# A decoder layer on one core: three sets of transposes moved from TensorE to VectorE's 32x32 turns and the stores behind them

## The chip, the core and the metric

The kernel runs on one core of a Trainium2 chip. The metric is the device time of one execution in microseconds, median of several runs. A core has TensorE (PE; its weight loads are listed as PEld), VectorE (DVE), ScalarE (ACT), GpSimd (POOL), and SyncE (SP), which here only issues DMAs. All data lie in SBUF, in PSUM (where TensorE writes) or in the chip's HBM. All arithmetic is float32; a product of float32 operands is made of three products of rounded parts (high times high, high times low, low times high).

## The reference, cut to what matters

One decoder layer, sequence 1024, width 1024. One projection feeds two groups of heads; their outputs are joined, projected, added to the input, and followed by a squared-ReLU MLP.

```python
h = rms_norm(x, norm1_w); proj = h @ w_in
# group A: 4 heads of differential attention, values of 128
da_o = (softmax(q1 k1^T) - lam * softmax(q2 k2^T)) v
da_o = rms_norm(da_o, da_out_norm_w) * (1.0 - lam_init)
# group B: 4 heads of the gated delta rule on convolved q, k, v (128 each)
dn_o = gated_delta_rule(dn_q, dn_k, dn_v, g, beta)
dn_o = rms_norm(dn_o, dn_out_norm_w) * silu(dn_z)
mix = concatenate([da_o, dn_o])            # (1024 tokens, 512 + 512)
x = x + mix @ w_out
x = x + square(relu(rms_norm(x, norm2_w) @ w_up)) @ w_down
```

## The kernel before

Tokens are cut into 8 tiles (or chunks) of 128. A matrix that is the operand of a projection is kept with features on partitions and tokens along them, as a rounded high part `hH` and a remainder `hL`, both [128, 8, 1024]. So whatever is computed with tokens on partitions has to be turned before a projection, and the other way round.

**Delta rule, projections** (50 to 250 us). `dn_proj(kind)` makes keys, queries and values, in this order, with features on partitions and 512 tokens at a time, convolves them on VectorE (L682) and yields 8 groups (4 heads, 2 halves). For the values (L851 to L857), `transposed` turns a group by four TensorE transposes into a bank of PSUM (L716); VectorE multiplies it by a factor of each token, `vsc`, on the way out (L854), and `park` stores it into slot 2 of the HBM tensor `park_d` with one DMA on SP. Between these groups, `horner` inverts the triangular matrices; its `V.transpose` (L806) turns 32x32 blocks.

**Delta rule, scan** (250 to 350 us). `scan` runs over the 8 chunks. `load` brings slots 0 to 2 of `park_d` for four heads into the tile `pka`, of which there are two, so the loads run about a chunk ahead. Each chunk is a chain: product with the state (L918), VectorE's combination with the values in slot 2 (L922), product with the inverse (L930), ScalarE's copy (L932), product for the new state (L941), VectorE's update (L947). In chunk 0 the values go into L930 directly. `scan_out` makes the chunk's output: two products (L970, L977), then mean square, power (L291 on GpSimd), gate and norm (L989), and a store to `mixn_d` from GpSimd's queue (L991). The gate comes in the tile `zgt`, of which there is one.

**Order of work.** In the scan, the attention and the output projection, TensorE's instructions keep the order in which the program issues them. That order is made by a planner, `Interleave`: generators (`scan`, `values`, `scores`, `da_turns`, `da_units`, `mixed`, `outproj` and others) each yield the time at which their next step should be ready and the bank of PSUM that they need, and the planner runs, of those that are ready, the one of highest priority. Its clock advances by given costs of TensorE (`flow.pe`), and `flow.chain` reckons when a row of instructions on the other engines will be done; `flow.hold` marks a bank as taken until then. The orders of the other engines and of the DMA queues are chosen by the compiler's scheduler. The scan starts at 18 us of the planner's clock; the projections of the attention (`da_units`) fill TensorE around it, and `da_turns` turns their rows.

**Attention** (350 to 580 us). For head and token tile, `scores` makes the exponentials, and `values` turns them (L1238), multiplies them with the values (L1250) into a bank of the pair `px`, copies the result (L1259), squares it into the same bank (L1260), and scales it (L1264) by mean square and weight. Heads 0 and 1 run over all tiles first and store each [128, 128] block to `mixa_d` from GpSimd's queue (L1266). Heads 2 and 3 follow tile by tile, and write into a row tile `mx` whose first half is loaded from `mixa_d` (L1231).

**Towards the output projection.** `mix_loads` loads the delta rule's rows into the tile `mt` (L1295), and `mixed` takes each row tile, of either group, through `turn` and `to_hT`: four TensorE transposes into a bank of `px` (L298), ScalarE's rounding into `hH` (L303), VectorE's remainder into `hL` (L304). `outproj` multiplies the delta rule's half and then the attention's (L1340 to L1342). The MLP follows and isn't touched.

Of the kernel before, what the change touches and what calls it, by code (L numbers as in the profile page):

```python
# [18 lines left out]
P = 128  # L19
# [96 lines left out]
def powr(n):  # L116
    return "G", 180.0 + 285.0 * n
# [3 lines left out]
def tile_hymba_layer(  # L121
# [46 lines left out]

    zg_d = dram.tile([NT, P, 512], F32, name="zg_d")
    park_d = dram.tile([HEADS, NT, P, 5, P], F32, name="park_d")  # L170
    mixn_d = dram.tile([NT, P, 512], F32, name="mixn_d")
    mixa_d = dram.tile([NT, P, 256], F32, name="mixa_d")
    fsx_d = dram.tile([P, 1024], F32, name="fsx_d")
    fsg_d = dram.tile([P, 1024], F32, name="fsg_d")
    qk_d = dram.tile([2, 2, NT, P, 2, 2 * P], F32, name="qk_d")
# [525 lines left out]
    def park(h, hf, slot, src):  # L701
        nc.sync.dma_start(park_d[h, 4 * hf:4 * hf + 4, :, slot, :].rearrange("c p d -> p c d"), v4(src))

    def cols4(t, h, hf):
        return t[:, 8 * h + 4 * hf:8 * h + 4 * hf + 4]

    def bc_col(t):
        return t.unsqueeze(2).broadcast_to([P, 4, P])
# [4 lines left out]
    def transposed(src):  # L713
        ps = pt_.tile([P, 512], F32, tag="pt", name="ps_t")
        for c in range(4):
            T.transpose(ps[:, c * P:(c + 1) * P], src[:, c * P:(c + 1) * P], ident)  # L716
        return ps
# [131 lines left out]

    heads = [((h, h + 1), hf) for hf in range(2) for h in (0, 2)]  # L850
    for h, hf, v2 in skew(dn_proj(2)):  # L851
        ps = transposed(v2)
        vs = ta("kn", 2)
        V.tensor_tensor(v4(vs), v4(ps), bc_col(cols4(vsc, h, hf)), ALU.mult)  # L854
        park(h, hf, 2, vs)
        if hf == 0:
            horner(*heads.pop(0))  # L857

# [43 lines left out]
    def scan():  # L902
        St = {}
        psA = pA.tile([P, 512], F32, name="ps_A")
        PA = {h: psA[:, h * P:(h + 1) * P] for h in range(HEADS)}

        def load(c):
            pka = sb.tile([P, HEADS, 3, P], F32, tag="pka", name="pka", bufs=2)
            for h in range(HEADS):
                nc.sync.dma_start(pka[:, h], park_d[h, c, :, 0:3, :])  # L910
            return pka

        nxt = load(0)
        for c in range(NT):
            pk, rr_, yy = nxt, {}, {}
            if c > 0:
                for h in range(HEADS):
                    T.matmul(PA[h], pk[:, h, 0, :], St[h], start=True, stop=True)  # L918
                for h in range(HEADS):
                    i = cidx(h, c)  # L920
                    rr_[h] = sb.tile([P, P], F32, tag="sr", name="sr", bufs=4)
                    V.scalar_tensor_tensor(rr_[h], PA[h], neg_eg[:, i:i + 1], pk[:, h, 2, :], ALU.mult, ALU.add)  # L922
                flow.pe(4 * MM)
                yield flow.chain(*[vec(P, 60)] * 4), None
            else:
                for h in range(HEADS):
                    rr_[h] = pk[:, h, 2, :]
            for h in range(HEADS):
                Wc = W[h, c // 4][:, (c % 4) * P:(c % 4 + 1) * P]
                T.matmul(PA[h], Wc, rr_[h], start=True, stop=True)  # L930
            y4 = sb.tile([P, 512], F32, tag="sy", name="sy", bufs=2)
            S.copy(y4, psA)  # L932
            if c + 1 < NT:
                nxt = load(c + 1)
            flow.pe(4 * MM)
            yield flow.chain(act(512)), None
            Sold = dict(St)
            for h in range(HEADS):
                yy[h] = y4[:, h * P:(h + 1) * P]
                if c < NT - 1:  # L940
                    T.matmul(PA[h], pk[:, h, 1, :], yy[h], start=True, stop=True)  # L941
            if c < NT - 1:
                for h in range(HEADS):
                    i = cidx(h, c)
                    Sn = sb.tile([P, P], F32, tag=f"S{h}", name=f"S{h}", bufs=2)
                    if c > 0:
                        V.scalar_tensor_tensor(Sn, St[h], elast[:, i:i + 1], PA[h], ALU.mult, ALU.add)  # L947
                    else:
                        V.tensor_copy(Sn, PA[h])
                    St[h] = Sn  # L950
                flow.pe(4 * MM)
            flow.add(1, scan_out(c, Sold, yy), 0, "pB")
            if c < NT - 1:
                yield flow.chain(*[vec(P, 60)] * 4), None

    def scan_out(c, Sold, yy):
# [29 lines left out]
        rstd(f, so, 1.0 / P, EPS, sb, "oft", 4)  # L986
        V.tensor_tensor(f, f, rq[:, c::8], ALU.mult)
        for h in range(HEADS):
            V.scalar_tensor_tensor(oc[:, h * P:(h + 1) * P], oc[:, h * P:(h + 1) * P], f[:, h:h + 1],  # L989
                                   zgt[:, h * P:(h + 1) * P], ALU.mult, ALU.mult)  # L990
        nc.gpsimd.dma_start(mixn_d[c], oc)  # L991
        flow.pe(4 * MM)
        t = flow.chain(vec(512))
        flow.hold("pB", t)
        flow.chain(*[act(P, True)] * 4, vec(4), powr(4), vec(4), *[vec(P, 60)] * 4, start=t)
        if c == NT - 1:
            s2ctx.close()
            spctx.close()
# [223 lines left out]
    def values():  # L1222
        for _ in order:
# [40 lines left out]
            V.scalar_tensor_tensor(om, om, f, dawb, ALU.mult, ALU.mult)  # L1264
# [5 lines left out]
            t = flow.chain(act(P, True), vec(1), powr(1), vec(1), vec(P, 60), start=t)  # L1270
# [5 lines left out]
    landed, hns = {}, {}  # L1276

    def turn(r, src, t, tb, k0, keep=None):
        to_hT(src, tb, lambda: bank_tile(px, r, "ps_tr"), k0, 4, keep)
# [638 lines left out]
```

## Time and profile before

| | |
|---|---|
| median of 3 runs | 1234.14 us (1233.48 to 1234.69) |
| the profiled execution | 1234.74 us, span 1233.0 us |
| granted clock of TensorE | 1.000 |
| DMA packets, bytes | 143301, 202.12 MB |
| HBM read, written | 135.86 MB, 65.01 MB |

The profile is of one execution. Its span runs from the first to the last instruction; the execution's own time has 1.7 us around it. The page gives the busy time of each engine, the chain of work that ended last (followed back from the last instruction, at each step to what released it), and groups of instructions by line. In the answers of the trace, a row such as "DVE STREAM_TRANSPOSE W<-gb x8: 690/702/712" gives the engine, the operation, the tile written and the one read, the count, and the least, median and greatest duration in ns. Rows of the chain and of the timeline begin with the start and the duration in us.

### The profile page before, as it was taken

To read this page: it belongs to the slowest core of one execution; us is meant where nothing else is said; L and a number is where in the kernel's file an instruction comes from. 1 tells how busy PE (TensorE), PEld (TensorE's weight loads), DVE (VectorE), ACT (ScalarE), POOL (GpSimd) and SP (SyncE) were. 2 spreads that over 40 slices of the span, in tenths; PEclk is the share of its full clock that TensorE was granted. 3 is DMA by queue.
4 is the path that set the end of the run, shared out by engine and by line. 5 is a ranking of instruction groups with operands and counts; after the bars stand their busy time and mean duration, and the time that the engine had idled before them with its cause. 6 is when DMAs were issued, how large, how long until landed. Compare 5 with 4: busy or idle time off the path is not lost.

```text
span 1233.0 us, 18819 instructions
## 1 busy us (share of the span) xinstructions
PE 1217.3 (99%) x6823; PEld 1054.3 (86%) x6823; DVE 824.7 (67%) x1524; ACT 624.2 (51%) x1249; POOL 151.3 (12%) x215
## 2 busy tenths in 40 slices
PE   9999999999999999999999999999999999999998
PEld 8978888898999998888888888888888888888886
DVE  6868796556647657777799544565569755777543
ACT  6588553344346555566666544444564333333330
POOL 2411110043434421001200000000000000000000
PEclk9999999999999999999999999999999999999999
DMA  9344653278748756323437434444479645423301
GB/s 350 98 115 122 163 162 104 63 234 240 231 148 252 232 162 159 85 77 108 157 117 255 172 122 151 171 170 153 155 241 382 234 179 184 163 103 103 137 35 69
DMA packets 143301, 202.12 MB, mean 164 GB/s; under 512 B 20920, under 2 KB 98280, under 8 KB 143208
## 3 DMA queue, kind: packets, MB, share of 16 engines
q1 hardware_dynamic: 138584, 187.28, 46.9%
q0 software_dynamic: 4480, 13.64, 2.9%
q8 instruction: 54, 0.88, 0.3%
q14 instruction: 39, 0.32, 0.1%
q10 hardware_dynamic: 144, 0.00, 0.0%
HBM read 135.86 MB, written 65.01 MB: 163 GB/s over the span
## 4 chain that ended last, share of the span: by engine, by line
PE 88%; DVE 4%; DMA 3%; ACT 2%; issue 2%; POOL 1%; SPq 1%; POOLq 0%; DVEq 0%; ACTq 0%
PE X L1517 4%; PE X L1515 4%; PE X L1516 4%; PE X L1814 4%; PE X L1815 4%; PE X L1813 4%; PE ps_dn L265 3%; PE ps_dn L267 3%; PE ps_dn L266 3%; PE ps_qk L1067 3%; PE ps_qk L1068 3%; PE ps_qk L1069 3%; PE ps_o L1250 2%; PE Y L1515 2%; PE Y L1517 2%; PE Y L1516 2%
## 5 line engine op out<-in xcount | busy, mean ns | idle before, releaser
L1433 ACT CAST hH<-ur 128x1024 fp32r<-128x1024 f32 x56 | 58.9, 1051 | 173.4 <-PE Y L1814 89.8
L1434 DVE TENSOR_TENSOR hL<-ur,hH 128x1024 fp32r<-128x1024 f32 x56 | 68.3, 1223 | 79.4 <-ACT hH L1433 79.4
L1067 PE MATMUL ps_qk<-wH,hH 128*128 128x256 f32 x384 | 114.3, 298 | 0.0
L1069 PE MATMUL ps_qk<-wH,hL 128*128 128x256 f32 x384 | 108.7, 283 | 0.0
L1068 PE MATMUL ps_qk<-wL,hH 128*128 128x256 f32 x384 | 108.4, 282 | 0.0
L1434 DVE TENSOR_TENSOR op<-raw,op 128x1024 fp32r<-128x1024 f32 x48 | 58.7, 1223 | 74.2 <-PE X L1516 41.1
L1813 PE MATMUL X<-hH 128*128 128x512 f32 x224 | 87.1, 389 | 0.0
L1814 PE MATMUL X<-hL,hH 128*128 128x512 f32 x224 | 87.1, 389 | 0.0
L1815 PE MATMUL X<-hH,hL 128*128 128x512 f32 x224 | 87.1, 389 | 0.0
L265 PE MATMUL ps_dn<-hH,wH 128*128 128x512 f32 x192 | 76.3, 397 | 0.2 <-ACT cp L678 0.2
L267 PE MATMUL ps_dn<-hH,wL 128*128 128x512 f32 x192 | 75.8, 396 | 0.0
L266 PE MATMUL ps_dn<-hL,wH 128*128 128x512 f32 x192 | 75.8, 395 | 0.0
L1068 PEld LDWEIGHTS ps_qk<-wL,hH 128*128 128x128 f32 x384 | 73.4, 191 | 0.2
L1067 PEld LDWEIGHTS ps_qk<-wH,hH 128*128 128x128 f32 x384 | 73.3, 191 | 0.2
L1069 PEld LDWEIGHTS ps_qk<-wH,hL 128*128 128x128 f32 x384 | 73.1, 190 | 0.0
L1434 DVE TENSOR_TENSOR hL<-dw,hH 128x1024 fp32r<-128x1024 f32 x56 | 68.2, 1218 | 0.9 <-ACT hH L1433 0.9
L1433 ACT CAST op<-raw 128x1024 fp32r<-128x1024 f32 x48 | 50.4, 1052 | 35.7 <-PE Y L1517 19.9
L1433 ACT CAST hH<-dw 128x1024 fp32r<-128x1024 f32 x56 | 58.7, 1048 | 10.7 <-DMA dw<-in_w_down_dram 5.0
L1205 ACT ACTIVATE pexp<-pexp,mx 128x128 f32<-128x128 f32 (+7 forms) x64 | 49.7, 777 | 25.1 <-DVE mx L1204 24.5
L682 DVE SCALAR_TENSOR_TENSOR cy<-cp,pv,cy 128x512 f32<-128x512 f32 x72 | 53.7, 747 | 8.1 <-ACT cy L680 7.3
L1340 PE MATMUL ps_op<-wH,hH 128*128 128x512 f32 x128 | 53.0, 414 | 0.0
L1515 PE MATMUL Y<-hH,op 128*128 128x512 f32 x128 | 49.9, 390 | 0.4 <-DVE ua L1555 0.4
(370 smaller groups left out, 3429.1 us busy)
## 6 DMA issues: line engine op xcount, KB each, us to landing
ur<-ud SPq DMA_DIRECT2D x28, 1024.0 KB, 5.0
raw<-in_w_up_dram SPq DMA_DIRECT2D x32, 512.0 KB, 3.9
dw<-in_w_down_dram SPq DMA_DIRECT2D x32, 512.0 KB, 6.8
wraw<-in_w_units_dram SPq DMA_DIRECT2D x48, 256.0 KB, 3.7
qk_d<-qa POOLq DMA_DIRECT2D x32, 256.0 KB, 4.3
ud<-ua SPq DMA_DIRECT2D x16, 512.0 KB, 4.2
ud<-s SPq DMA_DIRECT2D x16, 512.0 KB, 2.7
pka<-park_d SPq DMA_DIRECT2D x32, 192.0 KB, 4.8
```

What stands on the lines that cost most here:

```text
L265: T.matmul(ps, lh(k), rh(k), start=(k == 0), stop=False)
L266: T.matmul(ps, lh(k), rl(k), start=False, stop=False)
L267: T.matmul(ps, ll(k), rh(k), start=False, stop=(k == n - 1))
L1067: T.matmul(ps[:, :256], hH[:, k, sl], wh[:, k, :], start=(k == 0), stop=False)
L1068: T.matmul(ps[:, :256], hH[:, k, sl], wl[:, k, :], start=False, stop=False)
L1069: T.matmul(ps[:, :256], hL[:, k, sl], wh[:, k, :], start=False, stop=(k == KB - 1))
L1433: S.copy(dst[0], src)
L1434: V.tensor_tensor(dst[1], src, dst[0].bitcast(F32), ALU.subtract)
L1515: T.matmul(ps, op[0][:, k, cs], h[0][:, k, :], start=start and k == 0, stop=False, skip_group_check=True)
L1813: T.matmul(bank[t], v[0][:, j, sl], v[2][:, j], start=s0, stop=False, skip_group_check=True)
L1814: T.matmul(bank[t], v[0][:, j, sl], v[3][:, j], start=False, stop=False, skip_group_check=True)
L1815: T.matmul(bank[t], v[1][:, j, sl], v[2][:, j], start=False, stop=s1, skip_group_check=True)
```

## The change

Three sets of results are turned on VectorE in blocks of 32x32, and a store of four DMAs places the blocks, so that HBM holds the turned matrix.

- Values of the delta rule: `V.transpose` on the group, then `put_blocks` into slot 2 of `park_d`. The factor `vsc` is no longer applied here; GpSimd applies it in the scan, to the loaded tile (`scale`).
- Outputs of the delta rule: L989's result goes into `zgt`, is turned back into `oc`, and stored by `put_blocks` in `mixn_d`, which now has features by tokens. The load brings it with features on partitions, and `settle` rounds it straight into `hH` and `hL`, without a bank or TensorE.
- Attention heads 0 and 1: the scaled block is written into the product's bank, turned from there into `om`, and stored by `put_blocks` in `mixa_d` (features by tokens). When a row tile is complete, `turn_last` rounds its first half directly and turns only the second (heads 2 and 3) on TensorE.
- `put_blocks` issues four DMAs on SP, one for each 32 partitions, in pieces of 32 floats. The stores of `oc` and `om` were on GpSimd's queue before.
- The planner's chains are lengthened by the new VectorE steps; for heads 2 and 3 the bank is now also held through the square.

```diff
-    mixn_d = dram.tile([NT, P, 512], F32, name="mixn_d")
-    mixa_d = dram.tile([NT, P, 256], F32, name="mixa_d")
+    mixn_d = dram.tile([NT, 512, P], F32, name="mixn_d")
+    mixa_d = dram.tile([NT, 256, P], F32, name="mixa_d")
...
+    def put_blocks(dst, src, eng=None):
+        for a in range(4):
+            s = slice(32 * a, 32 * a + 32)
+            (eng or nc.sync).dma_start(dst[:, s].rearrange("(b s) r -> s b r", s=32),
+                                       src[s].rearrange("s (b r) -> s b r", r=32))
...
     for h, hf, v2 in skew(dn_proj(2)):
-        ps = transposed(v2)
         vs = ta("kn", 2)
-        V.tensor_tensor(v4(vs), v4(ps), bc_col(cols4(vsc, h, hf)), ALU.mult)
-        park(h, hf, 2, vs)
+        V.transpose(vs, v2)
+        put_blocks(park_d[h, 4 * hf:4 * hf + 4, :, 2, :].rearrange("c p d -> (c p) d"), vs)
...
+        def scale(c, pk):
+            G.tensor_tensor(pk[:, :, 2, :], pk[:, :, 2, :], bc_col(vsc[:, c::8]), ALU.mult)
+
         nxt = load(0)
+        scale(0, nxt)
...
             flow.add(1, scan_out(c, Sold, yy), 0, "pB")
+            if c + 1 < NT:
+                scale(c + 1, nxt)
...
         for h in range(HEADS):
-            V.scalar_tensor_tensor(oc[:, h * P:(h + 1) * P], oc[:, h * P:(h + 1) * P], f[:, h:h + 1],
-                                   zgt[:, h * P:(h + 1) * P], ALU.mult, ALU.mult)
-        nc.gpsimd.dma_start(mixn_d[c], oc)
+            hs = slice(h * P, (h + 1) * P)
+            V.scalar_tensor_tensor(zgt[:, hs], oc[:, hs], f[:, h:h + 1], zgt[:, hs], ALU.mult, ALU.mult)
+        V.transpose(oc, zgt)
+        put_blocks(mixn_d[c], oc)
...
-                nc.sync.dma_start(rows_of[tb][:, 0:256], mixa_d[tb])
+                nc.sync.dma_start(rows_of[tb][:, 0:256].rearrange("p (k t) -> p k t", k=2),
+                                  mixa_d[tb].rearrange("(k p) t -> p k t", p=P))
...
-            V.scalar_tensor_tensor(om, om, f, dawb, ALU.mult, ALU.mult)
-            if h < 2:
-                nc.gpsimd.dma_start(mixa_d[tb, :, h * P:(h + 1) * P], om)
             flow.pe((tb + 1) * MM)
             t = flow.chain(act(P))
+            if h < 2:
+                V.scalar_tensor_tensor(po[:, 2 * P:3 * P], om, f, dawb, ALU.mult, ALU.mult)
+                V.transpose(om, po[:, 2 * P:3 * P])
+                put_blocks(mixa_d[tb, h * P:(h + 1) * P], om)
+                flow.hold(r, flow.chain(act(P, True), vec(1), powr(1), vec(1), vec(P, 60), vec(P, 60), start=t))
+                continue
+            V.scalar_tensor_tensor(om, om, f, dawb, ALU.mult, ALU.mult)
+            t = flow.chain(act(P, True), start=t)
             flow.hold(r, t)
...
+    def settle(src, tb, ks, t=None):
+        sl = slice(tb * P, (tb + 1) * P)
+        sv = src.rearrange("p (k t) -> p k t", t=P)
+        S.copy(hH[:, ks, sl], sv)
+        V.tensor_tensor(hL[:, ks, sl], sv, hH[:, ks, sl].bitcast(F32), ALU.subtract)
...
+    def turn_last(r, src, t, tb):
+        settle(src[:, 0:256], tb, slice(0, 2))
+        ps = bank_tile(px, r, "ps_tr")
+        for j in (2, 3):
+            T.transpose(ps[:, j * P:(j + 1) * P], src[:, j * P:(j + 1) * P], ident)
+        flow.pe(2 * TR)
+        t = settle(ps[:, 256:512], tb, slice(2, 4))
...
-                nc.sync.dma_start(mt, mixn_d[t])
+                nc.sync.dma_start(mt.rearrange("p (k t) -> p k t", t=P), mixn_d[t].rearrange("(k p) t -> p k t", p=P))
...
+            if x[3] == 4:
+                loads.remove(x)
+                landed[x[2], 4] = settle(x[0], x[2], slice(4, 8))
+                state["mixed"] += 1
+                continue
             r = yield from flow.bank("px")
             loads.remove(x)
-            turn(r, *x)
-            state["mixed"] += x[3] == 4
+            turn_last(r, *x[:3])
```

More of the change, by code (lines that the diff above doesn't have):

```diff
@@ L994, in scan_out @@
         flow.hold("pB", t)
-        flow.chain(*[act(P, True)] * 4, vec(4), powr(4), vec(4), *[vec(P, 60)] * 4, start=t)
+        flow.chain(*[act(P, True)] * 4, vec(4), powr(4), vec(4), *[vec(P, 60)] * 4, vec(512, 100), start=t)
         if c == NT - 1:
@@ L1263, in values @@
             V.tensor_tensor(f, f, ri[:, 0:1], ALU.mult)
-            V.scalar_tensor_tensor(om, om, f, dawb, ALU.mult, ALU.mult)
-            if h < 2:
-                nc.gpsimd.dma_start(mixa_d[tb, :, h * P:(h + 1) * P], om)
             flow.pe((tb + 1) * MM)
             t = flow.chain(act(P))
+            if h < 2:
[6 more added lines that the diff above has]
+            t = flow.chain(act(P, True), start=t)
             flow.hold(r, t)
-            t = flow.chain(act(P, True), vec(1), powr(1), vec(1), vec(P, 60), start=t)
+            t = flow.chain(vec(1), powr(1), vec(1), vec(P, 60), start=t)
             if h == 3:
@@ L1276, in tile_hymba_layer @@
     landed, hns = {}, {}
+    def settle(src, tb, ks, t=None):
[3 more added lines that the diff above has]
+        V.tensor_tensor(hL[:, ks, sl], sv, hH[:, ks, sl].bitcast(F32), ALU.subtract)
+        n = P * (ks.stop - ks.start)
+        return flow.chain(act(n), vec(n), start=t)
+    def turn_last(r, src, t, tb):
[5 more added lines that the diff above has]
+        t = settle(ps[:, 256:512], tb, slice(2, 4))
+        flow.hold(r, t)
+        landed[tb, 0] = t
     def turn(r, src, t, tb, k0, keep=None):
```

## The prediction

> **What bounds the kernel now.** I read the page first (busy shares, then the chain that ended last), then the stretches, then the waits of TensorE alone, then the groups of instructions that the change removes or adds.
>
> ```profile
> span 1233.0 us, 18819 instructions
> PE 1217.3 (99%) x6823; PEld 1054.3 (86%) x6823; DVE 824.7 (67%) x1524; ACT 624.2 (51%) x1249; POOL 151.3 (12%) x215
> PE 88%; DVE 4%; DMA 3%; ACT 2%; issue 2%; POOL 1%; SPq 1%; POOLq 0%; DVEq 0%; ACTq 0%
> ```
>
> TensorE is busy for 99% of the span, but a busy PE in this profile only means that its pipeline isn't empty. The chain says more: 88% of the time that set the end is TensorE itself. The stretches are those of the change: the value projections (188 to 250 us), the scan of the delta rule (250 to 350), two attention heads (350 to 500), the other two with the output projection (500 to 585). In each row PE comes first, then PEld, DVE, ACT, POOL, the clock, the DMA share and GB/s.
>
> ```profile
> 188.00:250.00 62.00, 61.53 (x455) 53.95 (x453) 37.75 (x67) 19.91 (x42) 2.83 (x3) 1.00 0.30 82
> 250.00:350.00 100.00, 96.56 (x839) 95.22 (x838) 60.64 (x184) 44.13 (x133) 38.35 (x49) 1.00 0.75 233
> 350.00:500.00 150.00, 148.35 (x1105) 140.75 (x1105) 98.22 (x273) 88.59 (x232) 52.00 (x77) 1.00 0.66 190
> 500.00:585.00 85.00, 83.89 (x512) 73.50 (x512) 61.90 (x182) 54.46 (x153) 9.28 (x17) 1.00 0.30 88
> ...
> PEld ps_at L1238 <- ACT ps_o L1260: 2.0, 4, 1.1
> PEld ps_qkt L1028 <- ACT ps_o L1260: 1.6, 2, 1.1
> PEld ps_o L970 <- DMA pkb<-park_d: 1.4, 1, 1.4
> ```
>
> TensorE has work nearly all the time in all four; the scan has most idle time, 3.4 us of 100. Its waits by cause are small: six for a bank of PSUM that ScalarE's square at L1260 still holds (3.6 us) and one for a load of the scan (1.4 us). VectorE stands at 61 to 73% in these stretches. So an instruction taken off TensorE shortens the time by the part of the queue that it held, and one added to VectorE, GpSimd or a DMA queue costs nothing unless TensorE comes to wait for it. TensorE's order is fixed when the program is built, so it can't step around a late operand.
>
> **What leaves TensorE.** Three sets of transposes go: all four of each value group at L716, all four of each delta rule tile at L298, and two of the four of each attention tile there.
>
> ```profile
> L716 PE MATMUL ps_t<-ident,cth x32: 270/272/329, 141.9 to 240.9; 128*128 128x128 f32 x32
> L298 PE MATMUL ps_tr<-ident,mt x32: 270/272/273, 431.3 to 459.1; 128*128 128x128 f32 x32
> L298 PE MATMUL ps_tr<-ident,mx x32: 270/272/273, 517.4 to 582.5; 128*128 128x128 f32 x32
> ...
> 200.88 0.44 PE ps_t L716 x4
> 211.34 0.59 PE ps_t L716 x4
> 431.46 0.44 PE ps_tr L298 x4
> 582.38 0.44 PE ps_tr L298 x4
> ```
>
> The first three rows count them. The row of cth holds the second halves of queries and values, 16 each (their first halves have another buffer's name), so the values have 32 in 8 groups of four; the tile mt has 32, all to go; mx has 32, of which 16 go. One lasts 272 ns, but they overlap: in the chain, four take 0.44 us, 0.59 where the next product has to fill the pipeline again. That price counts, not 272 ns. Values: 8 groups at 0.44 to 0.59, 3.5 to 4.7 us, I take 4.0. Delta rule: 8 at 0.44 = 3.5 us. Attention: half of 8 at 0.44 = 1.8 us. **Sum: 9.3 us less (8.8 to 10.0)**, all of it on the chain, since these are rows of the chain.
>
> **What VectorE gets.**
>
> ```profile
> L806 DVE STREAM_TRANSPOSE W<-gb x8: 690/702/712, 196.8 to 241.4; 128x512 f32<-128x512 f32 x8
> L854 DVE TENSOR_TENSOR kn<-ps_t,vsc x8: 650/683/692, 190.1 to 242.0; 128x512 f32<-128x512 f32 x8
> ```
>
> The kernel already turns 32x32 blocks on VectorE: 702 ns for 128x512. For the values this replaces the 683 ns scaling, so nothing changes. Delta rule: 8 new ones, 5.6 us in a scan where VectorE is 61% busy. Attention: 16 of 128x128; such a width isn't shown, by share 702/4 = 176 ns, and the 128-wide rows below take 350; 2.8 to 5.6 us over 150 us. The rounding to high and low halves splits eight 512-wide pairs into sixteen 256-wide ones: a few us on two engines with room. Off the path: 0. [...]
>
> **Bank of PSUM in the two heads.** The product's bank is now kept through mean, power, scaling and turn.
>
> ```profile
> 395.47 0.19 ACT L1260 ACTIVATION_READ_ACCUMULATOR ps_o<-om,ri 128x1 f32 x1
> 396.18 0.57 POOL L291 TENSOR_TENSOR of<-oft,neghalf 128x1 f32<-128x1 f32 x1 [1.57 <-DVE oft L290]
> 397.61 0.35 DVE L1264 SCALAR_TENSOR_TENSOR om<-om,of,dawb 128x128 f32<-128x128 f32 x1
> ```
>
> Before, the bank is free at 395.66; after, at 397.96 plus a turn of 0.18 to 0.35: 2.5 to 2.7 us later, 16 times. The planner's chain counts these steps, so other work (projections until 460 us, output projection behind) should be put there. It also counts the square now, which the six waits above show it had left out. Bounds: 3.6 us better (those waits go) to 16 x 2.6 = 42 us worse (nothing covers). As the rows show waits of at most 1.1 us on this very release, I take 1 us worse.
>
> **Queues and DMAs.** Each store becomes four, with 128 B packets, all on SP; those of tiles oc and om leave GpSimd's queue.
>
> ```profile
> L702 SPq DMA_DIRECT2D park_d<-kn x16: 370/378/642, 90.2 to 242.7; - x16
> L804 SPq DMA_DIRECT2D gb<-fsg_d x32: 319/430/1815, 192.2 to 223.9; - x32
> L991 POOL DMA_DIRECT2D mixn_d<-oc x8: 539/539/602, 270.7 to 354.2; - x8
> SPq L962 <- DVE oc L989: 9.5, 4, 4.0
> ...
> DMA packets 546, 0.06 MB, mean 35 GB/s; under 512 B 546, under 2 KB 546, under 8 KB 546
> q1 hardware_dynamic: 546, 0.06, 23.2%
> ```
>
> An issue on SP takes 0.38 to 0.43 us: 32 for the values instead of 8, 32 in the scan, 64 in the heads, some 1.7 us for each set of four. In the scan SP waits for VectorE's oc already, four times, before it loads the next gate tile (L962), so a store that waits there is queued at a place where SP stands still anyway; behind it are the gate tile, park rows and weights, and who would wait for these are TensorE's L918 and L970. GpSimd's queue loses 8 issues of 0.54 us and 16 like them. The last two rows are from 198.7 to 200.5 us, when only 128 B loads ran: 23.2% of 16 engines x 1.8 us / 546 = 12.2 ns a packet. A set of 2048 takes 2048 x 12.2 / 16 = 1.6 us of all engines; in a chunk of the scan (12 us, engines 75% busy) this fits.
>
> **GpSimd's scaling** now stands between the scan's load and its use.
>
> ```profile
> L1370 POOL TENSOR_TENSOR hn<-hn,w2b x4: 1284/1290/1707, 586.0 to 606.8; 128x512 f32<-128x512 f32 x4
> DMA to landing us min/median/max: 2.4/4.8/6.4
> 249.42 3.66 SPq L910 DMA_DIRECT2D pka<-park_d  x8
> 254.97 0.77 POOL L1034 DMA_DIRECT2D qk_d<-qa  x1 [6.29 <-DVE qa L1033]
> 255.97 1.02 POOL L291 TENSOR_TENSOR rn<-rnt,neghalf 128x4 f32<-128x4 f32 x1 [0.23 <-DVE rnt L290]
> 256.45 0.97 PEld L930 LDWEIGHTS ps_A<-pka,W 128*128 128x128 f32 x8
> 308.23 1.80 SPq L910 DMA_DIRECT2D pka<-park_d  x4
> 322.57 0.35 DVE L922 SCALAR_TENSOR_TENSOR sr<-ps_A,neg_eg,pka 128x128 f32<-128x128 f32 x1 [1.91 <-PE ps_A L918]
> ```
>
> A multiply of this size takes 1.29 us on GpSimd (first row; the second is the landing of tile pka). Chunk 0: the first four of eight loads are issued by 251.2 and land by 255.6 at the median; scaled behind one issue (ends 255.74) that gives 257.0, behind the power too 258.3; TensorE wants the tile at 256.45. So 0 to 1.9 us late; I take 1.0. Later chunks are loaded a chunk ahead: chunk 6 is issued by 310.03, lands by 314.8 (316.4 at most) and VectorE first uses it at 322.57: 6.2 to 7.7 us of room for 1.29 us, or 3.1 behind one issue and one power. Cost 0, unless GpSimd stands at the scaling while powers queue behind it: those feed da_turns on TensorE. For this and the store queue together I take 1 us, of 0 to 13 (next part).
>
> **Sum against the profiled execution** (1234.74 us; the median of the runs is 1234.14, 0.6 less): 1234.7 - 9.3 + 1 + 1 + 1 = 1228.4, as a median 1227.8, so **1228 us**.
>
> **Rivals.**
> *The scan's operands come late (slower).* Per chunk the path load, scale, use grows by four issues (1.7), the stores' share of the DMA engines (1.6) and scaling (1.3 to 3.1): 4.6 to 6.4 us, against at least 6.2 of room. It decides from there. Where the load also lands at the slowest of its row, 6.4 instead of 4.8, the path is 8.0 us longer and each of seven chunks holds TensorE 1.8 us: 12.6 us, 1228 + 12.6 = 1241. To lose more than the gain it needs some 1.3 us a chunk. For it: SP and the DMAs are fullest here (0.75). Against: the room in the row, and pieces that overlap. [...] Chance 0.13.
> *The bank (slower still).* If half of the 2.6 us is uncovered in each of 16 blocks, 21 us: 1248. For it: TensorE meets this release six times already. Against: the plan knows it. From 0.55 us a block on, the gain is lost. Chance 0.08.
> *Gain given back.* TensorE arrives earlier and waits for operands whose times are set elsewhere (loads, powers); with other stalls of 9 us in the replanned order: 1234. Chance 0.12.
> *All of it and the waits.* 9.3 to 10 and 3.6 us: 1221. Chance 0.07, within faster.
>
> **How the numbers follow.** Forecast 0.60, with its own range 1223 to 1231.5; with the last rival faster 0.67; same 0.12; slower 0.21. The bound is 0.2%, 2.5 us, about what a measurement here can tell. The range takes in the full gain with the waits (1221) and the late scan (1241); outside are the bank and whatever is worse.
>
> **What would show it.** Right: 80 matmuls fewer, chain pieces L716 for values and L298 for mt gone, TensorE's end of each stretch earlier by 4, 3.5 and 1.8 us. Wrong: PEld waits on GpSimd's scaling or pka loads near L930 and L918 (the scan), or ps_at and ps_qkt waiting for VectorE's turn (the bank), of over 9 us in sum; or SP rows in which loads wait long for the turn. A VectorE wait that ends TensorE's idle time anywhere else would mean that I misread its room.

## The result: slower, not faster

The changed kernel takes 1254.54 us (median of 4 runs, 1252.17 to 1256.44); beside it the kernel before took 1233.93 us. The ratio is 1.0165, 95% interval 1.0147 to 1.0184: 20.6 us slower, where 1228 us were forecast and 1241 us was the upper end of the range. The profiled execution took 1256.44 us.

### The profile after

First the page: span, busy time of the engines, the clock that TensorE was granted in 40 slices, and the chain that ended last.

```profile
span 1254.7 us, 18831 instructions
PE 1219.8 (97%) x6743; PEld 1053.1 (84%) x6743; DVE 837.2 (67%) x1556; ACT 624.2 (50%) x1257; POOL 146.7 (12%) x199
PEclk9999999999999998999989999999999999999999
PE 86%; DMA 5%; DVE 3%; ACT 2%; issue 2%; SPq 1%; POOL 1%; DVEq 0%; POOLq 0%; ACTq 0%
```

80 matmuls are gone (6823 to 6743), as the change says. The engines that got the work are hardly busier: VectorE still stands at 67%, GpSimd at 12%. But TensorE is busy for 97% instead of 99%, DMA has 5% of the chain instead of 3%, and the row of the clock, which had no 8 before, has two. Next the stretches; the first four are those shown before, with PE first and the clock after POOL.

```profile
188.00:250.00 62.00, 61.53 (x462) 53.34 (x461) 38.69 (x69) 21.09 (x44) 2.13 (x3) 1.00 0.43 87
250.00:350.00 100.00, 92.82 (x775) 91.77 (x776) 62.68 (x178) 42.12 (x125) 41.59 (x49) 0.98 0.78 221
350.00:500.00 150.00, 137.41 (x1001) 129.31 (x1000) 95.65 (x277) 81.32 (x219) 42.82 (x59) 0.95 0.66 186
500.00:585.00 85.00, 83.84 (x500) 73.45 (x499) 61.36 (x164) 49.85 (x132) 6.58 (x12) 1.00 0.29 83
...
300.00:325.00 25.00, 24.89 (x198) 24.75 (x199) 17.88 (x49) 11.63 (x34) 10.57 (x12) 0.93 0.82 224
475.00:500.00 25.00, 19.04 (x92) 15.48 (x93) 15.03 (x36) 10.22 (x22) 1.10 (x2) 0.86 0.52 127
625.00:650.00 25.00, 20.91 (x96) 16.80 (x95) 21.08 (x39) 16.69 (x34) 2.18 (x3) 0.86 0.57 187
```

The values' stretch is as full as before, and it holds more matmuls of what follows (462 for 455). The scan has 92.8 us of TensorE in 100 instead of 96.6, the first two heads 137.4 in 150 instead of 148.3. In five stretches of 25 us the clock is below 1.00; three of them are shown (the others, 350 to 375 and 400 to 425 us, are at 0.93). What TensorE waits for (the line of the waiting product, what it waits for, us in total, times, longest):

```profile
PE ps_qkt L1041 <- DVE qn L1105: 5.1, 4, 1.6
PE ps_sc L1206 <- DMA qa<-qk_d: 3.4, 2, 1.9
PE ps_tr L1487 <- DVE nrt L290: 3.2, 1, 3.2
PE ps_sc L1207 <- DMA qb<-qk_d: 3.2, 2, 3.0
PE ps_o L982 <- DMA pkb<-park_d: 2.1, 1, 2.1
PE ps_at L1252 <- DVE ri L1226: 2.1, 1, 2.1
```

No single wait is large. There are many of 1 to 3 us: for the normed queries and keys (qn), for loads of queries (qa, qb) and of parked rows (pkb), for the softmax. And the rows of the new work:

```profile
L1003 DVE STREAM_TRANSPOSE oc<-zgt 128x512 f32<-128x512 f32 x8 | 5.6, 704 | 0.0
L1282 DVE STREAM_TRANSPOSE om<-ps_o 128x128 f32<-128x128 f32 x16 | 5.0, 313 | 0.4 <-DVE ps_o L1281 0.2
L920 POOL TENSOR_TENSOR pka<-pka,vsc 128x512 f32<-128x512 f32 x8 | 8.4, 1047 | 33.2 <-DMA pka<-park_d 30.4 <-DVE rnt L290 2.9
```

The prices per instruction were forecast well for the turns, 704 ns for 512 columns (702) and 313 ns for 128 (176 to 350), and too high for a multiply on GpSimd, 1047 ns (1290). The third row holds what was not: GpSimd stood idle for 33.2 us in front of its eight scalings, 30.4 of it for the load.

### Where the 20.6 us are

From the records of TensorE I added up the time in which neither a matmul nor a weight load ran: 9.5 us before, 28.2 us after, 18.7 more. The clock adds to that. At half clock (granted 0.5 in the trace) it stood for 3.4 us at 302, 370 and 411 us and for 6.8 us at 493 and 633 us, 23.9 us in all (0.07 and 0.14 of 25 us in the rows above say the same); before, only at the very end, behind the last product. These are products of one shape around 301.9 us, by the timeline (start, then duration):

```profile
301.53 0.28 PE L1080 MATMUL ps_qk<-wH,hH 128*128 128x256 f32 x1
301.65 0.28 PE L1081 MATMUL ps_qk<-wL,hH 128*128 128x256 f32 x1
...
302.29 0.42 PE L1082 MATMUL ps_qk<-wH,hL 128*128 128x256 f32 x1
302.50 0.42 PE L1080 MATMUL ps_qk<-wH,hH 128*128 128x256 f32 x1
```

They start every 0.12 us, then every 0.21: at half clock these products lose 43% of the time. By this I estimate the loss in all 23.9 us at some 10 us (at most, since idle time within these stretches is counted among the waits already). So 18.7 of waits, some 10 of clock, less the 9.3 us of transposes: 19.4, against 21.7 us in the span.

In time, the losses lie as follows. Each column gives by how much a landmark of TensorE ends later than before, in us, in the profiled execution of each kernel: the last value projection, the last product of the scan's chain (with the inverse, L930), the last query or key projection of the attention, and the first product of the MLP (before: 231.2, 339.0, 458.9, 615.4 us).

| kernel | values | scan | projections | MLP begins |
|---|---|---|---|---|
| after | -4.7 | +6.5 | +7.2 | +21.9 |
| v_only: the values' part alone | -4.8 | +10.0 | +10.3 | +10.2 |
| v_fold: the same, scale folded | -4.9 | -1.4 | -1.3 | -1.5 |
| n_oldplan: outputs alone, order kept | +0.2 | +2.8 | +1.3 | +1.5 |
| a_oldplan: heads alone, order kept | -0.3 | +0.3 | +19.6 | +22.5 |
| a_sbuf: the same, bank free as before | +0.2 | +1.2 | +1.5 | +4.3 |
| newplan: the order alone, nothing moved | +0.2 | +1.1 | +3.9 | +10.1 |
| combo: all three so | -4.9 | +1.5 | +0.5 | +2.9 |

The gain of the values' transposes is there, and of the forecast size, at the end of the value projections. Some 0.7 us of the -4.7 to -4.9 are not its own: the first 59 us, which no change touches, are that much shorter in these four executions; 4.0 to 4.2 us remain. In the changed kernel 11.2 us are lost in the scan, and another 14.7 between the last projection and the MLP. Differences of 1 to 2 us between rows can't be read: the kernel before itself took 1235.3 to 1236.5 us on the other chips of the experiments. The experiments below separate the causes.

### The profile page after: what moved, and what is told of

It is laid out like the page before. It is cut to its first block, busy times and chain, and to the rows that moved or that the text cites. A ratio compares the mean times of both kernels' runs of the same rounds, so it can differ in the third digit from the quotient of the medians.

```text
span 1254.7 us, 18831 instructions
## 1 busy us (share of the span) xinstructions
PE 1219.8 (97%) x6743; PEld 1053.1 (84%) x6743; DVE 837.2 (67%) x1556; ACT 624.2 (50%) x1257; POOL 146.7 (12%) x199
## 4 chain that ended last, share of the span: by engine, by line
PE 86%; DMA 5%; DVE 3%; ACT 2%; issue 2%; SPq 1%; POOL 1%; DVEq 0%; POOLq 0%; ACTq 0%
PE X L1556 5%; PE X L1557 5%; PE X L1558 5%; PE X L1854 4%; PE X L1856 4%; PE X L1855 4%; PE ps_dn L265 3%; PE ps_dn L267 3%; PE ps_dn L266 3%; PE ps_qk L1080 3%; PE ps_qk L1082 3%; PE ps_qk L1081 3%; PE Y L1557 2%; PE Y L1558 2%; PE Y L1556 2%; PE Z L1854 2%
## 5 line engine op out<-in xcount | busy, mean ns | idle before, releaser
L1474 ACT CAST hH<-dw 128x1024 fp32r<-128x1024 f32 x56 | 58.6, 1047 | 10.2 <-DMA dw<-in_w_down_dram 4.6
L1383 PE MATMUL ps_op<-wH,hL 128*128 128x512 f32 x128 | 51.0, 398 | 0.0
```

Source lines behind the costliest of these rows:

```text
L1474: S.copy(dst[0], src)
```

## The experiments

Sixteen kernels ran. Ratios are to the kernel before, run on the same chip beside each group, with 95% intervals; 0.001 is 1.2 us. "Order kept" means that the planner is told the figures of before, so that from the scan on TensorE's order is the one of before less the transposes.

### The parts alone, and the stores on the other queue

**v_only** has the values' hunks of the diff alone, **n_only** those of the delta rule's outputs, **a_only** those of heads 0 and 1. **full_pool** is the whole change with the stores of outputs and heads on GpSimd's queue:

```diff
-        put_blocks(mixn_d[c], oc)
+        put_blocks(mixn_d[c], oc, nc.gpsimd)
...
-                put_blocks(mixa_d[tb, h * P:(h + 1) * P], om)
+                put_blocks(mixa_d[tb, h * P:(h + 1) * P], om, nc.gpsimd)
```

> Only the values of the delta rule are turned in blocks (four stores on SP, GpSimd scales in the scan); the other two sets stay on TensorE. Theory 1 (in the attention heads, four small stores for each block wait in SP's queue ahead of the loads of q rows; TensorE idles for them, and after idle times of some us its clock is halved for a while): 3.5 to 4 us faster than before, 1230, clock 1.00. Theory 2 (the scan's operands come late, by the scaling and the stores): slower, 1236 to 1242, with idle time of TensorE between 250 and 350 us. Theory 3 (any new order of TensorE costs, whatever moves): 1238 to 1250, with the idle time anywhere behind 250 us.

> Only the outputs of the delta rule are turned in blocks. Theory 1: 0 to 3.5 us faster, 1231 to 1234, clock 1.00. Theory 2: 1236 to 1242, idle time of TensorE in the scan, behind loads of pkb. Theory 3: 1238 to 1250.

> Only the rows of attention heads 0 and 1 are turned in blocks. Theory 1: 8 to 18 us slower, 1242 to 1252, with stretches of halved clock between 360 and 500 us, and SP issues of mixa_d in front of the late loads of qa and qb. Theory 2: 1.8 us faster, 1232. Theory 3: 1238 to 1250.

> The whole change, but the stores of mixn_d and mixa_d are issued from GpSimd's queue, where they were before, in their four small pieces; the planner's order of TensorE is that of the changed kernel. Theory 1: most of the loss is gone, 1226 to 1236. Theory 2: the scan stays late, 1244 to 1254 (the stores take as much of the DMA engines). Theory 3: 1248 to 1256, as the order is the same.

Measured: v_only 1242.50 us, 1.0058 (1.0043 to 1.0073); n_only 1237.46, 1.0014 (1.0004 to 1.0023); a_only 1247.24, 1.0093 (1.0078 to 1.0108); full_pool 1256.33, 1.0166 (1.0149 to 1.0183). Each part alone is slower, by 7.2, 1.7 and 11.5 us, and the three add up to 20.4, the loss of the whole (each has an order of its own, so this sum doesn't show that they are independent). Moving the stores changed nothing in the whole; that this isn't because stores are free came out later.

The timeline of v_only shows how the scaling comes to hold TensorE (GpSimd, then VectorE, then TensorE):

```profile
317.40 1.04 POOL L920 TENSOR_TENSOR pka<-pka,vsc 128x512 f32<-128x512 f32 x1 [3.50 <-DMA pka<-park_d]
318.39 0.58 POOL L1003 DMA_DIRECT2D mixn_d<-oc  x1
319.00 1.03 POOL L291 TENSOR_TENSOR rn<-rnt,neghalf 128x4 f32<-128x4 f32 x1
...
320.06 0.43 DVE L1104 TENSOR_TENSOR qn<-qn,rn 128x256 f32<-128x256 f32 x1 [2.52 <-POOL rn L291]
...
320.55 0.48 PE L1040 MATMUL ps_qkt<-ident,qn 128*128 128x128 f32 x1 [3.68 <-DVE qn L1104]
```

GpSimd stands for 3.5 us until the tile of the next chunk lands, scales it (1.04 us), issues a store (0.58 us), and only then, at 319.00 us, takes the power for a norm of the attention's queries. VectorE waits for that power, TensorE for VectorE, 3.68 us, and from 319.0 us on the clock is at half for 6.8 us (mean of the profiled execution 0.995). The scaled tile itself is in little hurry: the longest that TensorE waits for one is 0.5 us, at the first chunk. Another chain pays, one that has nothing to do with the scan.

### The scaling

**v_noscale** is v_only without `scale` (it leaves the factor out, so its values are unscaled); **v_dve** has it on VectorE; **v_fold** applies the factor where it meets no load, to the columns of the inverse and, inverted, to the factor of the running sum:

```diff
+            V.tensor_tensor(v4(z[h]), v4(z[h]), bc_col(cols4(vsc, h, hf)), ALU.mult)
             W[h, hf] = z[h]
...
+    negr = sp.tile([P, 32], F32, name="negr")
+    V.reciprocal(negr, vsc)
+    V.tensor_tensor(negr, negr, neg_eg, ALU.mult)
...
-                    V.scalar_tensor_tensor(rr_[h], PA[h], neg_eg[:, i:i + 1], pk[:, h, 2, :], ALU.mult, ALU.add)
+                    V.scalar_tensor_tensor(rr_[h], PA[h], negr[:, i:i + 1], pk[:, h, 2, :], ALU.mult, ALU.add)
```

> The values' part alone, without the scaling by vsc (the factor is left out altogether, so the values are unscaled); the four small stores stay, TensorE's order is that of v_only. If GpSimd's scaling, which waits for the load with the powers of da_units queued behind it, is what costs: 3 to 5 us below before, 1230 to 1233, clock 1.00. If the small stores or the new order in the projections cost: 1240 to 1244 as v_only.

> v_only with the scaling on VectorE in place of GpSimd. If the place in GpSimd's queue costs: 1230 to 1236, as VectorE needs 0.7 us for it and the powers are free; if any wait for the load in a busy queue costs, VectorE's queue is held instead: 1238 to 1250. If stores or order cost: 1240 to 1244.

> The values part alone, turned in blocks and stored as in the change, but with the scale folded into two places where it meets no load: into the columns of the inverse W before they are stored (one 128x512 multiply on VectorE for each group of four chunks), and into the factor of the running sum (computed once). GpSimd's scaling in the scan is gone. Without any scaling this part was 2.9 us faster than before, with the scaling on GpSimd 7.2 us slower and on VectorE 11.5 us slower. If the wait of an in-order queue for the loaded tile is the cost: 1 to 4 us faster. If what costs is that the scaled values are needed at all (other data, eight more multiplies): 3 us or more slower. If the added 0.7 us of VectorE in the projections of the values holds the inverse up: no change.

Measured: v_noscale 1233.58 us, 0.9977 (0.9968 to 0.9986); v_dve 1247.99, 1.0092 (1.0075 to 1.0109); v_fold 1233.33, 0.9981 (0.9972 to 0.9990). So the scaling costs v_only some 10 us (7.2 slower against 2.8 faster) for 8.4 us of an engine that is busy for an eighth of the span. On VectorE it costs more, though each takes less; the group of v_dve (busy, mean ns, idle time in front):

```profile
L920 DVE TENSOR_TENSOR pka<-pka,vsc 128x512 f32<-128x512 f32 x8 | 5.5, 690 | 17.5 <-DMA pka<-park_d 17.5
```

VectorE, which has over five times the work of GpSimd, stands for 17.5 us. TensorE's waits for the normed rows, which need both engines, follow the scaling (before, v_only, v_noscale, v_dve):

```profile
PE ps_qkt L1028 <- DVE qn L1092: 1.3, 2, 1.0
...
PE ps_qkt L1040 <- DVE qn L1104: 8.3, 7, 3.7
...
PE ps_qkt L1034 <- DVE qn L1098: 1.3, 2, 1.0
...
PE ps_qkt L1040 <- DVE qn L1104: 12.4, 9, 4.6
```

Without the scaling they are as before. The price is that of the wait in the engine's queue, not of the multiply. Folded, the part is 2.3 us faster than before, with all its turns and small stores. Of the kernels that compute the whole layer, this is the one that beats both; it keeps a little over half of the 4.0 us forecast for the values.

### The bank, and the order that goes with it

**a_oldplan** is a_only with the order kept. **newplan** is the reverse: nothing is moved, but the planner is told a_only's figures, and so lays out its order. **a_sbuf** is a_oldplan with the scaled block written to a tile in SBUF, so that the bank is free after the square, as before:

```diff
-                V.scalar_tensor_tensor(po[:, 2 * P:3 * P], om, f, dawb, ALU.mult, ALU.mult)
-                V.transpose(om, po[:, 2 * P:3 * P])
+                ot = ap.tile([P, P], F32, tag="ot", name="ot", bufs=1)
+                V.scalar_tensor_tensor(ot, om, f, dawb, ALU.mult, ALU.mult)
+                V.transpose(om, ot)
```

> The attention part alone, as in a_only, but the planner is given the figures of the kernel before, so that TensorE's order is that of before less 16 transposes (checked instruction by instruction). If the work itself costs (the bank of PSUM is held longer, small stores): 1243 to 1250 as a_only, with more waits of TensorE on L1264's successor in the heads. If the new order costs: 1232 to 1236.

> The kernel before with nothing moved; only the planner gets the figures that a_only gives it, so that TensorE's order is that of a_only with the 16 transposes back in. If the new order costs: 1242 to 1250. If the work costs: 1233 to 1237.

> The attention part alone, with the order that the kernel before has less its 16 transposes (the planner's figures are those of before), and with the scaled block written to a tile in SBUF instead of to the product's bank; the turn reads that tile, so the bank is free after ScalarE's square again. The same work with the bank kept (old order) was 21 us slower than before. If the held bank is what the heads pay for: 1.8 us faster than before for the transposes that are gone, between 0 and 3 faster. If the turns on VectorE, the 64 small stores on SP's queue or the split rounding are what costs: still 7 us or more slower. If the order of before is simply too tight for four transposes fewer (operands late in other places): no change, or up to 4 us slower, with the waits of TensorE spread over other products.

Measured: a_oldplan 1257.80 us, 1.0177 (1.0162 to 1.0193); newplan 1245.47, 1.0075 (1.0060 to 1.0090); a_sbuf 1238.61, 1.0026 (1.0017 to 1.0036). In the old order the held bank costs 18.7 us (21.9 less 3.2): the two kernels differ in nothing else. a_oldplan lies above both of its expected ranges. The 3.2 us that a_sbuf is slower, where 1.8 faster would follow if the bank were all, are spread: TensorE's idle time is 13.2 us instead of 9.5, of which 1.6 is one load of queries at 490 us. One release in the timeline of a_oldplan, GpSimd, VectorE, TensorE:

```profile
373.82 1.32 POOL L291 TENSOR_TENSOR rn<-rnt,neghalf 128x4 f32<-128x4 f32 x1 [4.73 <-DVE oft L290]
375.13 0.54 POOL L291 TENSOR_TENSOR of<-oft,neghalf 128x1 f32<-128x1 f32 x1
...
375.18 0.42 DVE L1099 TENSOR_TENSOR qn<-qn,rn 128x256 f32<-128x256 f32 x1 [0.93 <-POOL rn L291]
375.70 0.16 DVE L1271 TENSOR_TENSOR of<-of,ri 128x1 f32<-128x1 f32 x1
375.90 0.36 DVE L1275 SCALAR_TENSOR_TENSOR ps_o<-om,of,dawb 128x128 f32<-128x128 f32 x1
376.29 0.32 DVE L1276 STREAM_TRANSPOSE om<-ps_o 128x128 f32<-128x128 f32 x1
...
376.76 0.45 PE L1035 MATMUL ps_qkt<-ident,qn 128*128 128x128 f32 x1 [5.03 <-DVE om L1276]
```

The bank's power waits for another power on GpSimd, its scaling for other work of VectorE: each step of the longer hold stands in a queue of its own. TensorE waits 5.03 us for the bank here, where six waits before were 1.1 us at most. The planner sees a longer hold and moves other work: a_only, planned anew, is 10 us better than a_oldplan. But the new order isn't free: newplan pays 9.3 us for it with no work moved. They are waits again: TensorE is idle for 17.7 us instead of 9.5, and 3.4 us at half clock (mean 0.998) add 1.5, estimated by the 43% above. Most of it is lost behind the last projection (+3.9 there, +10.1 at the MLP).

### The order and the outputs

**n_oldplan** is n_only with the order kept; **combo** joins v_fold, n_oldplan and a_sbuf, and so has none of the 80 transposes.

> The delta rule's outputs alone, with the planner's figures as before, so that TensorE's order is that of before less the 32 transposes (the change plans them anew). With the new order this part was 1.7 us slower than before. If the new order cost it its gain: 3.5 us faster than before, between 1.5 and 4.5. If VectorE's 0.7 us turns or the four stores in place of one make TensorE wait: no change or 2 us slower again. If the time that the transposes free is given back to the next waits (operands whose times are set elsewhere): within 1.5 us of before.

> The three parts together in these forms: the scale folded into the inverse and the sum's factor, the attention block scaled into SBUF, the planner's figures as before. All 80 transposes are gone, as in the change. If the change lost by the three mechanisms that these forms take away (a queue that waits for a load, a bank kept too long, a new order), the parts add up: 1236 less 6 to 9 us, about 1228. If each gain is given back to waits once TensorE runs ahead of the loads, or idle time of some us in one place halves the clock again: 1233 to 1240. If transposes on VectorE are what the time is lost to, whatever stands around them: slower than 1245.

Measured: n_oldplan 1235.77 us, 1.0002 (0.9993 to 1.0011); combo 1236.96, 1.0015 (1.0005 to 1.0025). The outputs' 3.5 us are given back in full, and combo, with all three mechanisms taken away, is 1.8 us slower than before, where 6 to 9 us faster would follow if they were all. TensorE's idle time in combo is 17.4 us (9.5 before), and a half clock of 3.4 us (mean 0.998) takes an estimated 1.5: 9.4 us, as much as the transposes gave. The largest wait is for the parked rows of a chunk, at 298.9 us, 3.64 us where before it was 1.21. The two DMA views, before and then combo, from 280 to 300 us:

```profile
DMA  8889998879998799940100389999999999999999
DMA packets 4707, 5.12 MB, mean 256 GB/s; under 512 B 384, under 2 KB 4016, under 8 KB 4706
KS<-qk_d SPq DMA_DIRECT2D x4, 256.0 KB, 5.0
pkb<-park_d SPq DMA_DIRECT2D x5, 128.0 KB, 5.3
```

```profile
DMA  8958899999999967786689999999999999998876
DMA packets 6662, 5.12 MB, mean 256 GB/s; under 512 B 2476, under 2 KB 6063, under 8 KB 6660
KS<-qk_d SPq DMA_DIRECT2D x4, 256.0 KB, 6.7
pkb<-park_d SPq DMA_DIRECT2D x4, 128.0 KB, 6.9
```

The same 5.12 MB go in 2000 more small packets, and the loads land 1.6 to 1.7 us later after their issue. Before, the engines (first row, busy tenths in slices of 0.5 us) had a gap of some 2 us from 289 us on; in combo they have none. The load for which TensorE waits is issued at 290.9 us in combo (292.4 before) and lands at 298.9 (298.5 before): TensorE is there 2.0 us earlier (295.3 for 297.3) and the rows are not. v_fold, without these small stores at this place, gives back less: it waits 2.5 us for the same rows.

### The whole change, cost by cost

**full_fold** is the changed kernel with v_fold's form for the scale; **full_fold_sbuf** also has a_sbuf's tile, and the planner's hold for it; both keep the changed planner otherwise. **combo_pool** and **a_sbuf_pool** are combo and a_sbuf with the stores of outputs and heads on GpSimd's queue, as in full_pool.

> The whole change with its own planner and order, only the scaling on GpSimd replaced by the scale folded into the inverse and the running sum's factor. The scaling cost some 10 us where the values were changed alone. If the three parts' losses add up, 1254.5 less 10: about 1245, between 1242 and 1248. If the bank or the new order set the waits and the scaling hides behind them: 1250 or more.

> The same, and the attention block scaled into a tile of its own in SBUF, so that the product's bank is free after the square; the planner keeps the changed figures for all else. What is left against the three-part version with the old planner (1237) is the new order. If the bank's hold itself costs some 10 us: about 1236. If the new order costs the rest (it cost 9 us on a kernel with nothing moved): 1242 to 1246.

> The three-part version (1237) with the small stores of the delta rule and of the heads on GpSimd's queue, where the kernel before has its two. In the three-part version TensorE waits 3.6 us for the parked rows of chunk 3 and about 1.1 us for queries, with four stores in front on SP. If SP's queue is where the missing gain went: 1229 to 1232. If the gain is given back to loads whatever queue the stores stand in: 1236 to 1238. If GpSimd, with 0.5 us for each issue, now holds up the powers of the norms: slower than 1239.

> The attention part with the tile in SBUF and the order of before (1238.6, 3.1 us slower than before), its stores on GpSimd's queue. If the four stores in front of a query load on SP (TensorE waits 1.6 us for it at 489.97 us) are the cause: 1234 to 1235.5. If the waits come from the shift of TensorE against its operands, or the turn on VectorE: 1238 again.

Measured: full_fold 1249.68 us, 1.0112 (1.0096 to 1.0127); full_fold_sbuf 1247.97, 1.0101 (1.0086 to 1.0115); combo_pool 1252.98, 1.0145 (1.0131 to 1.0159); a_sbuf_pool 1246.03, 1.0089 (1.0075 to 1.0103). From the change's 1.0165 down to combo's 1.0015: the scaling 0.0053 (6.5 us), the bank with the planner's figure for it 0.0011 (1.4 us, within the intervals of each other), the rest of the new order 0.0086 (10.6 us). I had expected 10 for the scaling, and either the bank or the order for the rest. The middle step isn't the bank alone, since the shorter hold also changes TensorE's order between 371 and 597 us. A cleaner pair is a_only and newplan: their products stand in the same order, one by one (the 16 transposes aside), and a_only, with the bank held and all its work moved, is 2.2 us slower, within the intervals of each other. So it is mostly the order: where the order reckons with the hold, the hold is covered, as the prediction counted on.

What the new order loses shows in full_fold_sbuf, in its longest wait of TensorE, with SP's queue ahead of it:

```profile
481.29 1.28 SPq L1129 DMA_DIRECT2D KS<-qk_d  x2
482.63 2.04 SPq L708 DMA_DIRECT2D mixa_d<-om  x4
484.76 2.21 SPq L1129 DMA_DIRECT2D KS<-qk_d  x2
487.01 0.63 SPq L1145 DMA_DIRECT2D qb<-qk_d  x1
...
490.37 0.79 PE L1205 MATMUL ps_sc<-KS,qb 128*128 128x512 f32 x1 [7.55 <-DMA qb<-qk_d]
```

The scores stand in TensorE's order at 482.8 us, but SP issues their load at 487.0, behind the keys of the next head and four small stores. The changed kernel has the same at 493 us (3.0 us), and half clock from there.

My expectation that GpSimd's queue is the better place for the stores fell in both kernels: it costs a_sbuf another 7.8 us and combo 16. TensorE's waits for normed rows (qn) are 10.2 us in combo_pool, 2.1 in combo. The timeline of combo_pool:

```profile
315.53 2.61 POOL L708 DMA_DIRECT2D mixn_d<-oc  x4 [3.23 <-DVE rnt L290]
318.15 1.03 POOL L291 TENSOR_TENSOR rn<-rnt,neghalf 128x4 f32<-128x4 f32 x1
...
319.21 0.43 DVE L1103 TENSOR_TENSOR qn<-qn,rn 128x256 f32<-128x256 f32 x1 [2.22 <-POOL rn L291]
...
319.69 0.47 PE L1039 MATMUL ps_qkt<-ident,qn 128*128 128x128 f32 x1 [3.26 <-DVE qn L1103]
```

Four issues take 2.61 us on GpSimd, the power waits behind them, and TensorE 3.26 us for the power: the chain of v_only with a store at its head. The time of the issues decides here, by what is queued behind it: the same transfers, 16 us apart.

## Why the prediction was wrong, by its own steps

Two terms of the sum failed: GpSimd's scaling (1 us; some 10 alone, 6.5 in the whole) and the bank with its plan (1 us; 18.7 where the plan doesn't know of the hold, a new order of some 9 to 11 us where it does). The gain itself was given back in part as well.

- **What leaves TensorE: right in size.** The last value projection ends 4.7 us earlier, 4.0 of it by the values as forecast, and 80 matmuls are gone. But "all of it on the chain" doesn't follow from the rows being in the chain: of 4.0 us v_noscale keeps 2.8 and v_fold 2.3, of 3.5 us for the outputs n_oldplan keeps none.
- **What VectorE gets, off the path: right in itself.** a_sbuf, n_oldplan and v_fold have all the turns between them, and the split rounding, and stand at +3.2, +0.2 and -2.3 us. Its room at 67% was no cover, though, for work that stands behind other work in its queue (a wait of 5.03 us for the bank in a_oldplan).
- **GpSimd's scaling with the stores' queue, 1 us of 0 to 13: mis-sized most.** The scaling alone is some 10 us (v_only against v_noscale), 6.5 in the whole (after against full_fold). The prediction named the way it happens, "GpSimd stands at the scaling while powers queue behind it", and gave it 1 us together with the stores' queue (its other 1 us, for the first chunk, was 0.5 in v_only). It looked at the room between load and use of the tile (6.2 to 7.7 us), and its first rival let TensorE wait at L918 and L930; neither is where it cost. What counted was when the load lands against when GpSimd reaches the instruction: in the changed kernel it stands for the load for 30.4 us.
- **The bank, 1 us of -3.6 to 42: failed.** I took the nearest row, a wait of 1.1 us for ScalarE's square, for a release that now lies behind GpSimd's power and VectorE's queue; they were not the same release. "The plan knows it" was true and no help: the hold costs 18.7 us in the old order, and little in the new one, which costs 9.3 by itself with nothing moved, 10.6 in the whole. The cost of a new order had no term in the sum.
- **Queues and DMAs.** Issue prices were near, 1.95 us for a set of four where 1.7 were forecast. That "a store that waits there is queued at a place where SP stands still anyway" held only for gate tiles; in the heads the stores stand in front of query loads. The small packets decided nothing at the values: v_noscale has their 32 small stores and is faster than before (0.9977). In the scan, loads land 1.6 to 1.7 us later among 2000 more small packets (combo); whether by their number, by their size or by their place in the queue, no run tells.
- **The clock** had no term. At most some 10 us of the loss are half clock behind waits; the trace before shows none to read this from.
- **Rivals.** "The scan's operands come late" was right about the place and the size in v_only, wrong about the way, and its price rests on a slip: the room of 6.2 us already has the load land as late as 6.4 us, and the path of 8.0 us adds that lateness once more. Counted once it is 6.4 against 6.2, or 8.0 against 7.7, at most 0.3 us a chunk and 1230 us in place of 1241, the upper end of the range. "The bank" had the mechanism; that its 21 us is near what a_oldplan measures (21.9) is luck, as TensorE waits for the turn six times there, 11.7 us in all, and not 1.3 us in each of 16 blocks, and half clock adds the rest. "Gain given back", at chance 0.12, is what n_oldplan and combo do. All three are true at once, and the prediction weighed them as if one would exclude the others. Of its signs of being wrong the last one came: waits of TensorE for VectorE elsewhere, 5.1 us for qn and 3.2 for nrt.

Not settled: how much of the new order's cost is the order of TensorE and how much the order of SP's loads that comes with it, since the one changes with the other; and 2.8 us of combo, whose span is 2.9 us longer where waits and clock less the transposes give 0.1 (up to 0.8 of it can be the chip, on which the kernel before took 1235.52 us).

## What to carry to other kernels

Before an instruction with a late operand is put on an engine that is nearly idle, look at what stands behind it in that engine's queue and who waits for that: here 8.4 us of work on an engine at 12% cost 10 us, by way of a norm in another stage. Find a form that meets no load (a factor folded into an operand that is already there) before a better engine for it. Where an order is planned, a change of the plan's figures is a change of its own: measure it with nothing moved, and measure the move with the order kept.

## What the runs showed of the hardware

In the changed kernel TensorE's granted clock fell to half five times before the last product: for 3.413 us at 301.9, 370.2 and 411.1 us, for 6.827 us at 493.0 and 633.0 us. The later four begin 20, 32, 56 and 97 times 3.413 us behind the first. In the 3.413 us ahead of each fall, neither a product nor a weight load ran for 1.62, 1.58, 2.08, 1.96 and 2.68 us; in the first half of the two longer ones for 2.98 and 0.86 us. The length of one wait doesn't tell: behind one of 1.56 us, at 288.4 us, the clock stayed full, while the 1.58 us ahead of the fall at 370.2 us were two waits, of 0.31 and 1.27 us. In the kernel before, no wait between the first product and the last is over 1.21 us, and the clock is full until 1231.9 us, 3.4 us behind the end of the last product. These two traces show no more of what sets the fall. At the 43% above, 3.413 us at half clock cost an estimated 1.5 us, here behind a single wait of 2.08 us at 408 us.

In the changed kernel the issues of the small blocked stores on SP took 0.43 us (median of 64, heads) and 0.49 us (median of 32, outputs); four together took 1.76 to 2.07 us between 455 and 500 us. On GpSimd, in combo_pool, the four of one chunk's outputs took 2.61 us at 315.5 us, 0.65 us each.
